# First four projection units regrouped by contraction tile, four outputs at once, two more units behind them

## Chip, cores and metric

One core of a Trainium2 chip runs the kernel. The time is that of one execution on the device in microseconds (us), as the median over runs of the same program. TensorE (PE) runs the matmuls; VectorE (DVE), ScalarE (ACT) and GpSimd (POOL) do the rest of the arithmetic, and SyncE (SP) issues the transfers from HBM.

## The reference, cut to what matters

Two requests of 256 tokens each (`x_prompt`, `x_sample`), model width 1024, pass a trunk of two layers in float32. The change touches the first steps of the layer: the RMS norm of the input and the projections of the mixers "a" (differential attention) and "b" (neighbourhood attention with a relative bias).

```python
def rmsnorm(x, g):
    x32 = x.astype(jnp.float32)
    y = x32 * lax.rsqrt(jnp.mean(x32 * x32, axis=-1, keepdims=True) + EPS)
    return (y * g.astype(jnp.float32)).astype(x.dtype)
...
    for l in range(DEPTH):
        h = rmsnorm(x, attn_norm[l])
        proj = h @ w_in[l]
        a_cols, b_cols, c_cols, d_cols, g_cols = jnp.split(proj, [p1, p2, p3, p4], axis=-1)
        ...
        o_b = natten_mixer(b_cols, b_rpb[l])
...
        x = x + merged @ w_out[l]
...
    return rmsnorm(x, final_norm)
```

## The kernel before

**Data.** x is kept transposed: eight tiles `x[d]` of 128 channels by 512 tokens (both requests side by side), all in `xall`. A projection contracts over these eight k-tiles. To keep float32 accuracy each product is made of three matmuls in the fp32r format (`mm3`, L295): high part of the weight times high part of x, high times low, low times high. `prep` (L320) makes the parts `xh` and `xl` of one tile with the norm's gain in them, `split_piece` (L278) those of the weights: ScalarE copies `raw` to `wh` (L288), VectorE makes the first half of `wl` (L291) and GpSimd the second (L292).

**Units.** The weights are laid out as a list of pieces (`_piece_order`, L128), and the main loop at the end of `trunk_kernel` goes through one unit for each piece. In layer 0 it starts bq0, bk0, bq1, bk1 (queries and keys of mixer b, 24 matmuls of 128x512 each), vb0, vb1 (values of b, whose 96 matmuls `psvb` follow in unit vb1), then aq0, ak0, aq1, ak1 and so on through gates, output projection and feed-forward. A unit's step emits its matmuls, then evacuations of earlier units, then the split of the piece two units ahead (`LOOK`) and the load of the piece three further (`RAW_BUFS`). Three buffers each stand for `raw`, `wh` and `wl`, so a piece's `wh` waits for the matmuls of the piece three before it.

**Side work.** Generators run between the units: `norm_gen` (L359) makes the norm's row: `st` (sum of squares by TensorE, L344), a chain of small steps `ms`, `ny`, `nt` on 128x4 (`newton`, L304), `rs`, the transposes `rb` (L357), and the copy `rsrow` (L372). The gain is in `xh`, but the row factor is applied when outputs are evacuated (`b_evac`, L596, makes `bc`, its high and low part; `a_evac`, L583, rotates with `cosr` and `sinr` as well, using a shuffle, GpSimd's `rsh`, and `rc`). `sq_acc` (L331) makes the squares, added up by VectorE. `bias_gen` (L698) loads the relative bias in 16 transfers and adds the mask on GpSimd (L704). `pair_gen` (L811) makes an attention pair: scores `sc` (L744), softmax on VectorE and ScalarE (`sb`, `mx`, `ri`), transposes `pt`, output `po`; the tables START, GAP and the lags say at which unit which step stands.

**Start.** SP loads x tile 0, the halves of piece 0, x tile 1, the halves of piece 1, the other x tiles in pairs, piece 2, and the constants (L1136 to L1144); nine matmuls on zeros (`warm`, L1131) run before the first weights are there. Piece 0's `wl` is made by GpSimd alone, piece 1's in quarters by both.

**PSUM.** Four banks (`pm`) for the units, two (`psx`) for scores, one (`pst`) for `pt`, one (`pso`) for `st`, `rb` and `po`.

**Order.** A scheduler orders the instructions of each engine; each engine then goes through its own in order, and an instruction whose wait isn't over holds all behind it on that engine.

Of the kernel before, what the change touches and what calls it, by code (L numbers as in the profile page):

```python
# [37 lines left out]
START = {"a": ("ak0", 7), "b": ("bk0", 4), "c": ("cv", 6), "d": ("vf1", 2)}  # L38
# [40 lines left out]
def _layout_weights(w_in, c_w_uq, c_w_ukv, w_branch, w_out, w_ffn_in, w_ffn_out):  # L79
# [5 lines left out]
    for l in range(DEPTH):  # L85
        p = {}
        for nm, cols in _col_blocks():
            a = kt(w_in[l][:, cols])
            if nm[0] == "v":
                p[nm + "0"] = a[:, 0:4]  # L90
                p[nm + "1"] = a[:, 4:8]
            else:
                p[nm] = a
        z = np.zeros((128, 2, 384), np.float32)
# [33 lines left out]
def _piece_order():  # L128
# [3 lines left out]
    names += qk[0] + [f"v{two_[0]}0", f"v{two_[0]}1"]  # L132
    rest = {"x": qk[1], "w": [f"v{two_[1]}0", f"v{two_[1]}1"], "d": ["vd0", "vd1", "ve0", "ve1"], "c": ["vf0", "vf1"]}
# [68 lines left out]
def trunk_kernel(ctx: ExitStack, tc: tile.TileContext, xt, wflat, gains, lams, rpb, consts, yt):  # L202
# [75 lines left out]
    def split_piece(i, parts=1, pool_only=False):  # L278
# [7 lines left out]
        for q in range(parts):  # L286
            a, b = q * w, q * w + w
            S.activation(out=wh[:, a:b], in_=raw[:, a:b], func=AF.Copy)  # L288
            c = a if pool_only else (a + b) // 2
            if c > a:  # L290
                V.tensor_tensor(out=wl[:, a:c], in0=raw[:, a:c], in1=f(wh[:, a:c]), op=ALU.subtract)  # L291
            G.tensor_tensor(out=wl[:, c:b], in0=raw[:, c:b], in1=f(wh[:, c:b]), op=ALU.subtract)  # L292
# [65 lines left out]

    def norm_gen(wait, rope):  # L359
# [6 lines left out]
        yield  # L366
        pb = psum("rb", pso)
# [62 lines left out]
    units = []  # L430
# [4 lines left out]
    def build_layer(l):  # L435
# [136 lines left out]
        def lin(nm, m=128):  # L572
            def pe(wh, wl):
                ps = psum("ps" + nm)
# [486 lines left out]
        for nm in ("aq0", "ak0", "aq1", "ak1"):  # L1061
            specs[nm] = (lin(nm), a_evac(nm))
# [4 lines left out]
        for nm in ("bq0", "bk0", "bq1", "bk1"):  # L1067
            specs[nm] = (lin(nm), b_evac(nm))
# [18 lines left out]
        at(1, bias_gen)  # L1087
# [24 lines left out]
        xw = 2 if l == 0 else 1  # L1112
        units[u0]["side"].append((0, lambda: norm_gen(xw, True)))
        for nm in names[:1 + xw]:
            units[u0 + pos[nm]]["nb"] = u0 + 1 + xw
# [157 lines left out]
```

## Time and profile before

| | |
|---|---|
| median of 3 runs | 1627.73 us (1627.72 to 1628.39) |
| profiled execution, own time | 1629.04 us |
| its span, first to last instruction | 1627.3 us |
| TensorE busy | 1610.2 us (99%) |
| VectorE busy | 962.9 us (59%) |
| ScalarE busy | 620.5 us (38%) |
| GpSimd busy | 661.2 us (41%) |
| mean granted TensorE clock | 0.995 |
| TensorE's share of the chain that ended last | 97% |

The span runs from the first to the last instruction of the profiled execution; its own time, measured outside, is 1.7 us longer. A granted clock of 1.00 is TensorE's upper level (2.4 GHz), 0.50 the lower (1.2 GHz). Matmuls overlap in the rows of the trace, so the distance between starts, not the listed duration, is what one costs. In the rows, "[3.39 <-ACT wh L288]" is the idle time of the engine just before the instruction and the instruction that ended it.

### The profile page before, as it was taken

Reading aid. Unit: us, or ns where it says so; the run is one execution under the profiler, and the core shown is the slowest. Engines: PE = TensorE matmul, PEld = TensorE weight load, DVE = VectorE, ACT = ScalarE, POOL = GpSimd, SP = SyncE. Lnnn points to the kernel's source line nnn. Section 1 sums busy time; section 2 is a strip of 40 time slices with the busy share of each in tenths; the row PEclk is TensorE's granted clock in tenths of the full one; section 3 lists DMA queues with packets and bytes.
Section 4 is the critical chain, followed back from the end, with each engine's and each line's share of the span. In section 5 each row is a group of like instructions: output and inputs, shape, how many; then the busy total and the mean of one; then the engine's idle time right before and its main releaser. Section 6 shows DMA issues by size and latency. Waiting matters only on the chain.

```text
span 1627.3 us, 21327 instructions
## 1 busy us (share of the span) xinstructions
PE 1610.2 (99%) x8163; PEld 1336.7 (82%) x8163; DVE 962.9 (59%) x1580; ACT 620.5 (38%) x1107; POOL 661.2 (41%) x449
## 2 busy tenths in 40 slices
PE   8999999999999999999999999999999999999997
PEld 6898788888888888888888977888788888888886
DVE  7767485656876665633366665756468656665113
ACT  4446354333333333322234555434332333333221
POOL 4432223445534444444445231244455344444342
PEclk9999999999999999999999999999999999999999
DMA  6213122221322322223332222222222222322331
GB/s 220 101 53 98 56 98 82 81 78 59 116 91 91 104 95 98 90 95 105 102 105 85 67 88 72 82 86 76 81 78 104 92 95 99 104 91 86 105 96 64
DMA packets 50534, 149.25 MB, mean 92 GB/s; under 512 B 13184, under 2 KB 16128, under 8 KB 50432
## 3 DMA queue, kind: packets, MB, share of 16 engines
q1 hardware_dynamic: 49344, 146.84, 26.8%
q8 instruction: 64, 1.05, 0.3%
q10 hardware_dynamic: 1088, 1.05, 0.2%
q14 instruction: 38, 0.31, 0.1%
HBM read 145.77 MB, written 2.10 MB: 91 GB/s over the span
## 4 chain that ended last, share of the span: by engine, by line
PE 97%; DVE 1%; ACT 1%; issue 1%; DMA 0%; POOL 0%; SPq 0%; POOLq 0%; ACTq 0%
PE pf L296 10%; PE pf L297 10%; PE pf L298 10%; PE pg L296 7%; PE pg L297 7%; PE pg L298 7%; PE pfo L296 5%; PE pfo L297 5%; PE pfo L298 5%; PE po L842 2%; PE pt L787 2%; PE pb L298 2%; PE pwo L296 2%; PE pb L297 2%; PE pb L296 2%; PE pwo L298 2%
## 5 line engine op out<-in xcount | busy, mean ns | idle before, releaser
L292 POOL TENSOR_TENSOR wl<-raw,wh 128x512 fp32r<-128x512 f32 (+4 forms) x264 | 454.4, 1723 | 567.6 <-ACT wh L288 466.6
L288 ACT ACTIVATE wh<-raw 128x1024 fp32r<-128x1024 f32 (+5 forms) x264 | 281.6, 1067 | 437.4 <-PE pfo L297 128.2
L291 DVE TENSOR_TENSOR wl<-raw,wh 128x512 fp32r<-128x512 f32 (+4 forms) x262 | 258.9, 988 | 227.6 <-ACT wh L288 209.8
L296 PE MATMUL pf<-xh,wh 128*128 128x512 f32 x704 | 274.3, 390 | 0.0
L298 PE MATMUL pf<-xh,wl 128*128 128x512 f32 x704 | 273.9, 389 | 0.0
L297 PE MATMUL pf<-xl,wh 128*128 128x512 f32 x704 | 273.9, 389 | 0.0
L296 PE MATMUL pg<-xh,wh 128*128 128x512 f32 x512 | 203.4, 397 | 0.4
L297 PE MATMUL pg<-xl,wh 128*128 128x512 f32 x512 | 199.7, 390 | 0.0
L298 PE MATMUL pg<-xh,wl 128*128 128x512 f32 x512 | 199.7, 390 | 0.0
L296 PEld LDWEIGHTS pf<-xh,wh 128*128 128x128 f32 x704 | 132.2, 188 | 27.4
L298 PEld LDWEIGHTS pf<-xh,wl 128*128 128x128 f32 x704 | 132.2, 188 | 27.4
L297 PEld LDWEIGHTS pf<-xl,wh 128*128 128x128 f32 x704 | 132.2, 188 | 27.3
L296 PE MATMUL pfo<-ah,wh 128*128 128x512 f32 (+1 forms) x374 | 141.1, 377 | 0.0
L297 PE MATMUL pfo<-al,wh 128*128 128x512 f32 (+1 forms) x374 | 140.8, 376 | 0.0
L298 PE MATMUL pfo<-ah,wl 128*128 128x512 f32 (+1 forms) x374 | 140.8, 376 | 0.0
L911 POOL TENSOR_TENSOR mg<-mg,gz 128x512 f32<-128x512 f32 x48 | 64.4, 1346 | 165.5 <-DVE gz L910 165.5
L302 POOL TENSOR_TENSOR al<-fc,ah 128x512 fp32r<-128x512 f32 x44 | 57.8, 1315 | 178.9 <-ACT ah L301 178.9
L296 PEld LDWEIGHTS pg<-xh,wh 128*128 128x128 f32 x512 | 96.2, 188 | 23.4 <-issue 1.3
L298 PEld LDWEIGHTS pg<-xh,wl 128*128 128x128 f32 x512 | 96.1, 188 | 20.7
L297 PEld LDWEIGHTS pg<-xl,wh 128*128 128x128 f32 x512 | 96.3, 188 | 18.4
L932 ACT ACTIVATE gz<-gz 128x512 f32<-128x512 f32 x64 | 40.3, 630 | 133.9 <-DVE gz L931 133.8
L767 ACT ACTIVATE pr<-sc,mx 128x256 f32<-128x256 f32 x128 | 59.0, 471 | 73.5 <-DVE mx L762 73.5
(386 smaller groups left out, 2841.5 us busy)
## 6 DMA issues: line engine op xcount, KB each, us to landing
raw<-in_w_dram SPq DMA_DIRECT2D x158, 512.0 KB, 3.2
raw<-in_w_dram SPq DMA_DIRECT2D x58, 640.0 KB, 3.8
raw<-in_w_dram SPq DMA_DIRECT2D x32, 448.0 KB, 3.2
raw<-in_w_dram SPq DMA_DIRECT2D x4, 576.0 KB, 3.3
bias<-in_rpb_dram SPq DMA_DIRECT2D x32, 64.0 KB, 3.0
xall<-in_xt_dram SPq DMA_DIRECT2D x3, 512.0 KB, 7.4
raw<-in_w_dram SPq DMA_DIRECT2D x4, 256.0 KB, 4.8
out_dram<-y SPq DMA_DIRECT2D x4, 256.0 KB, 2.4
```

The lines of the kernel that those rows point to most:

```text
L288: S.activation(out=wh[:, a:b], in_=raw[:, a:b], func=AF.Copy)
L291: V.tensor_tensor(out=wl[:, a:c], in0=raw[:, a:c], in1=f(wh[:, a:c]), op=ALU.subtract)
L292: G.tensor_tensor(out=wl[:, c:b], in0=raw[:, c:b], in1=f(wh[:, c:b]), op=ALU.subtract)
L296: PE.matmul(ps, lhsT=wh, rhs=xh, start=first, stop=False)
L297: PE.matmul(ps, lhsT=wh, rhs=xl, start=False, stop=False)
L298: PE.matmul(ps, lhsT=wl, rhs=xh, start=False, stop=last)
L302: (eng or V).tensor_tensor(out=l, in0=v, in1=f(h), op=ALU.subtract)
L767: S.activation(out=p[:, qt * 256:qt * 256 + 256], in_=src[c][:, qt * 256:qt * 256 + 256], func=AF.Exp, scale=sc, bias=mx[:, i:i + 1], accu ...
L787: PE.transpose(out=ps[:, kt * 256 + qt * 128:kt * 256 + qt * 128 + 128], in_=p[:, qt * 256 + kt * 128:qt * 256 + kt * 128 + 128], identity ...
L842: PE.matmul(ops[64 * e:64 * e + 64, :256], lhsT=v_of(mix, j, e, 2 * b + kt), rhs=pt[:, kt * 256:kt * 256 + 256], start=(kt == 0), stop=(kt ...
L911: G.tensor_tensor(out=m, in0=m, in1=z, op=ALU.add)
L932: S.activation(out=z, in_=z, func=AF.Tanh, scale=0.5)
```

## The change

The weights of bq0, bk0, bq1 and bk1 are laid out anew as four slabs. A slab holds two k-tiles of all four outputs (2 x 4 blocks of 128 columns), so that its 24 matmuls add to four PSUM banks in turn, and every k-tile of x is used for 12 matmuls as soon as it is there. Loads at the start alternate between a tile of x and half a slab, 256 KB each; cst comes in two transfers. aq0 and ak0 move up to right behind the slabs, with their outputs in `pst` and `pso`; vb0 and vb1 follow. Slabs 0 to 3 have their `wl` made by VectorE alone, in two halves. The squares are made at the start and added by VectorE into one sum. In layer 0 `norm_gen` is replaced by two hooks: `st` and the small chain at the last matmul of slab 3, `rb` and `rsrow` behind the sixth k-tile of aq0. All four outputs of the slabs are evacuated together. The bias moves from unit 1 to unit 4 in layer 0; the steps of the pairs of a and b move with START. Layer 1 has the same pieces and the same order of units, but keeps `norm_gen` and the bias at unit 1.

```diff
--- before.py
+++ after.py
@@ -35,7 +35,8 @@
 GAP = {"a": 3, "b": 2, "c": 2, "d": 3}
-START = {"a": ("ak0", 7), "b": ("bk0", 4), "c": ("cv", 6), "d": ("vf1", 2)}
+START = {"a": ("ak0", 9), "b": ("bk0", 5), "c": ("cv", 6), "d": ("vf1", 2)}
+SLAB = ["bq0", "bk0", "bq1", "bk1"]
 CLAG = 1
@@ -83,14 +84,18 @@
     for l in range(DEPTH):
-        p = {}
+        p, slab = {}, {}
         for nm, cols in _col_blocks():
...
                 p[nm + "1"] = a[:, 4:8]
+            elif nm in SLAB:
+                slab[nm] = a
             else:
                 p[nm] = a
+        for q, nm in enumerate(SLAB):
+            p[nm] = np.stack([slab[b][:, k] for k in (2 * q, 2 * q + 1) for b in SLAB], axis=1)
         z = np.zeros((128, 2, 384), np.float32)
@@ -129,8 +134,9 @@
     qk = [[f"{m}q0", f"{m}k0", f"{m}q1", f"{m}k1"] for m in two_]
-    names += qk[0] + [f"v{two_[0]}0", f"v{two_[0]}1"]
-    rest = {"x": qk[1], "w": [f"v{two_[1]}0", f"v{two_[1]}1"], "d": ["vd0", "vd1", "ve0", "ve1"], "c": ["vf0", "vf1"]}
+    assert qk[0] == SLAB
+    names += qk[0] + qk[1][:2] + [f"v{two_[0]}0", f"v{two_[0]}1"]
+    rest = {"x": qk[1][2:], "w": [f"v{two_[1]}0", f"v{two_[1]}1"], "d": ["vd0", "vd1", "ve0", "ve1"], "c": ["vf0", "vf1"]}
     for ch in 'xdcw':
@@ -275,7 +281,7 @@
 
-    def split_piece(i, parts=1, pool_only=False):
+    def split_piece(i, parts=1, only=None):
         if i >= len(order):
@@ -286,10 +292,11 @@
             S.activation(out=wh[:, a:b], in_=raw[:, a:b], func=AF.Copy)
-            c = a if pool_only else (a + b) // 2
+            c = b if only is V else (a + b) // 2
             if c > a:
                 V.tensor_tensor(out=wl[:, a:c], in0=raw[:, a:c], in1=f(wh[:, a:c]), op=ALU.subtract)
-            G.tensor_tensor(out=wl[:, c:b], in0=raw[:, c:b], in1=f(wh[:, c:b]), op=ALU.subtract)
+            if b > c:
+                G.tensor_tensor(out=wl[:, c:b], in0=raw[:, c:b], in1=f(wh[:, c:b]), op=ALU.subtract)
         splits[i] = (wh, wl)
@@ -356,6 +363,17 @@
 
+    def norm_parts(rope):
+        def stats():
+            ps = psum("st", pso)
+            main_stats(ps)
+            main_newton(ps)
+
+        def row():
+            for _ in norm_row(rope):
+                pass
+        return stats, row
+
     def norm_gen(wait, rope):
@@ -364,6 +382,9 @@
         yield
+        yield from norm_row(rope)
+
+    def norm_row(rope):
         pb = psum("rb", pso)
@@ -427,7 +448,7 @@
 
-    units = []
+    units, hooks = [], {}
 
@@ -569,15 +590,34 @@
 
-        def lin(nm, m=128):
+        def lin(nm, m=128, pool=pm):
             def pe(wh, wl):
-                ps = psum("ps" + nm)
+                ps = psum("ps" + nm, pool)
                 D[nm] = ps
...
                     mm3(ps[:m], w[0][:, k], w[1][:, k], st["xh"][k], st["xl"][k], k == 0, k == 7)
+                    if k == 5 and pool is pst and "row" in hooks:
+                        hooks.pop("row")()
+            return pe
+
+        def slab_pe(q):
+            def pe(wh, wl):
+                if q == 0:
+                    swap_h()
+                    for nm in SLAB:
+                        D[nm] = psum("ps" + nm)
+                w = [a[:, :1024].rearrange("p (k c) -> p k c", k=8) for a in (wh, wl)]
+                kb = [(k, b) for k in range(2) for b in range(4)]
+                if q == 3:
+                    kb.sort(key=lambda t: t[1])
+                for k, b in kb:
+                    d = 2 * q + k
+                    mm3(D[SLAB[b]], w[0][:, 4 * k + b], w[1][:, 4 * k + b], st["xh"][d], st["xl"][d], d == 0, d == 7)
+                    if q == 3 and (k, b) == (1, 3) and "stats" in hooks:
+                        hooks.pop("stats")()
             return pe
@@ -1059,13 +1099,14 @@
         for nm in ("aq0", "ak0", "aq1", "ak1"):
-            specs[nm] = (lin(nm), a_evac(nm))
+            specs[nm] = (lin(nm, pool={"aq0": pst, "ak0": pso}.get(nm, pm)), a_evac(nm))
         for nm, n, ev in (("va", 256, v_evac(vA)), ("vb", 256, v_evac(vB)), ("vd", 256, vd_evac), ("ve", 288, ve_evac),
...
             specs[nm + "0"], specs[nm + "1"] = (pe0, None), (pe1, None)
-        for nm in ("bq0", "bk0", "bq1", "bk1"):
-            specs[nm] = (lin(nm), b_evac(nm))
+        evs = [b_evac(nm) for nm in SLAB]
+        for q, nm in enumerate(SLAB):
+            specs[nm] = (slab_pe(q), (lambda: [e() for e in evs]) if q == 3 else None)
         specs["cq"] = (cq_pe, None)
@@ -1084,7 +1125,7 @@
 
-        at(1, bias_gen)
+        at(4 if l == 0 else 1, bias_gen)
         s = 0
@@ -1109,10 +1150,10 @@
         units[u0 + pos["fu0"]]["side"].append((0, lambda: norm_gen(1, False)))
-        xw = 2 if l == 0 else 1
-        units[u0]["side"].append((0, lambda: norm_gen(xw, True)))
-        for nm in names[:1 + xw]:
-            units[u0 + pos[nm]]["nb"] = u0 + 1 + xw
+        if l == 0:
+            hooks["stats"], hooks["row"] = norm_parts(True)
+        else:
+            units[u0]["side"].append((0, lambda: norm_gen(1, True)))
         units[u0 + pos["wo0"]]["nb"] = u0 + pos["wo1"] + 1
@@ -1133,32 +1174,46 @@
     xv = xt.rearrange("(d p) t -> p d t", p=128)
-    nc.sync.dma_start(out=xall[:, 0:1], in_=xv[:, 0:1])
-    load_piece(0, 2)
-    nc.sync.dma_start(out=xall[:, 1:2], in_=xv[:, 1:2])
-    load_piece(1, 2)
-    for a, b in ((2, 4), (4, 6), (6, 8)):
-        nc.sync.dma_start(out=xall[:, a:b], in_=xv[:, a:b])
-    load_piece(2)
-    nc.sync.dma_start(out=cst, in_=consts)
+
+    def load_slab(i):
+        raw = wpool.tile([128, 1280], F32, tag="raw", name=f"raw{i}", bufs=RAW_BUFS)
+        src = wflat[offs[i]:offs[i] + 128 * 1024].rearrange("(p n) -> p n", p=128)
+        for q in range(2):
+            d = 2 * i + q
+            nc.sync.dma_start(out=xall[:, d:d + 1], in_=xv[:, d:d + 1])
+            nc.sync.dma_start(out=raw[:, q * 512:q * 512 + 512], in_=src[:, q * 512:q * 512 + 512])
+        raws[i] = raw
+
+    for i in range(3):
+        load_slab(i)
+    nc.sync.dma_start(out=cst[:, K_ID:], in_=consts[:, K_ID:])
+    prep(0, gcol(0, G_ATTN), False)
+    split_piece(0, 2, V)
+    load_slab(3)
+    nc.sync.dma_start(out=cst[:, :K_ID], in_=consts[:, :K_ID])
     nc.sync.dma_start(out=lv, in_=lams.rearrange("(u n) -> u n", u=1).to_broadcast([128, DEPTH * L_ROW]))
-    prep(0, gcol(0, G_ATTN), False)
-    split_piece(0, 2, True)
-    load_piece(RAW_BUFS)
+    accs = []
+
+    def sq_start(d):
+        sq = t2(f"sq{d}")
+        S.activation(out=sq, in_=x[d], func=AF.Square)
+        if d:
+            V.tensor_tensor(out=accs[0], in0=accs[0], in1=sq, op=ALU.add)
+        else:
+            accs.append(sq)
+
     for d in range(1, ND):
-        prep(d, gcol(0, G_ATTN + d), False, d % 2 == 1)
+        prep(d, gcol(0, G_ATTN + d), False, True)
         if d == 2:
-            split_piece(1, 2)
+            split_piece(1, 2, V)
             load_piece(1 + RAW_BUFS)
-
-    def sq_gen():
-        for d in range(ND):
-            sq_acc(d, d)
-            if d in (2, 4):
-                yield
-        yield
-
-    units[0]["side"].insert(0, (0, sq_gen))
+        if d >= 3:
+            sq_start(d - 3)
+            if d == ND - 1:
+                for e in range(d - 2, ND):
+                    sq_start(e)
+    st["accs"] = accs
+
     for i in range(2, LOOK):
@@ -1206,7 +1261,7 @@
         vec(1)
-        split_piece(i + LOOK)
+        split_piece(i + LOOK, *((2, V) if i + LOOK < 4 else ()))
         load_piece(i + LOOK + RAW_BUFS)
```

The first place is TensorE at the first real matmuls. Names end in the piece or k-tile (`xh1` is the high part of the second tile of x, `wh0` that of piece 0) and, behind the underscore, a running number. Before:

```order
L296 MATMUL psbq0_180<-xh0_122,wh0_126 128x512
L297 MATMUL psbq0_180<-xl0_123,wh0_126 128x512
L296 MATMUL psbk0_247<-xh0_122,wh1_142 128x512
L297 MATMUL psbk0_247<-xl0_123,wh1_142 128x512
L298 MATMUL psbk0_247<-xh0_122,wl1_143 128x512
L296 MATMUL psbk0_247<-xh1_134,wh1_142 128x512
L298 MATMUL psbq0_180<-xh0_122,wl0_127 128x512
L296 MATMUL psbq0_180<-xh1_134,wh0_126 128x512
L297 MATMUL psbq0_180<-xl1_135,wh0_126 128x512
L298 MATMUL psbq0_180<-xh1_134,wl0_127 128x512
L297 MATMUL psbk0_247<-xl1_135,wh1_142 128x512
L298 MATMUL psbk0_247<-xh1_134,wl1_143 128x512
```

After the change:

```order
L303 MATMUL psbq0_199<-xh0_123,wh0_127 128x512
L304 MATMUL psbq0_199<-xl0_124,wh0_127 128x512
L303 MATMUL psbk0_200<-xh0_123,wh0_127 128x512
L304 MATMUL psbk0_200<-xl0_124,wh0_127 128x512
L305 MATMUL psbq0_199<-xh0_123,wl0_128 128x512
L305 MATMUL psbk0_200<-xh0_123,wl0_128 128x512
L303 MATMUL psbq1_201<-xh0_123,wh0_127 128x512
L304 MATMUL psbq1_201<-xl0_124,wh0_127 128x512
L305 MATMUL psbq1_201<-xh0_123,wl0_128 128x512
L303 MATMUL psbk1_202<-xh0_123,wh0_127 128x512
L304 MATMUL psbk1_202<-xl0_124,wh0_127 128x512
L305 MATMUL psbk1_202<-xh0_123,wl0_128 128x512
```

Before, the third matmul already needs piece 1 (`wh1`); now the first twelve use piece 0 and x tile 0 alone, over four outputs.

The second place is VectorE at the norm of layer 0, `wl` being halves of weight splits. Before, from the end of the small chain on:

```order
L352 COPY rs_330<-ny_315 128x4
L376 TENSOR_TENSOR rs2_371<-rs_330 128x4
L1173 TENSOR_REDUCE lp_395<-lv_84 128x1 x4
L291 TENSOR_TENSOR wl5_412<-raw5_216,wh5_411 128x512
L1177 TENSOR_TENSOR lam_85<-lp_395 128x1 x2
L1179 TENSOR_SCALAR lam_85<-lam_85 128x1 x2
L372 COPY rsrow_369<-rb_339 128x512
L601 TENSOR_TENSOR bc_377<-psbq0_180,rsrow_369 128x8x64
```

After the change, from inside the chain:

```order
L314 TENSOR_SCALAR ny_329<-ny_329 128x4
L318 TENSOR_TENSOR nt_330<-ny_329 128x4
L319 TENSOR_TENSOR nt_330<-nt_330,nh_331 128x4
L297 TENSOR_TENSOR wl6_456<-raw6_265,wh6_455 128x512
L320 SCALAR_TENSOR_TENSOR ny_329<-nt_330,ny_329 128x4
L318 TENSOR_TENSOR nt_330<-ny_329 128x4
L319 TENSOR_TENSOR nt_330<-nt_330,nh_331 128x4
L320 SCALAR_TENSOR_TENSOR ny_329<-nt_330,ny_329 128x4
```

and from its end:

```order
L1232 TENSOR_TENSOR lam_85<-lp_346 128x1 x2
L1234 TENSOR_SCALAR lam_85<-lam_85 128x1 x2
L297 TENSOR_TENSOR wl7_498<-raw7_296,wh7_497 128x512
L393 COPY rsrow_413<-rb_408 128x512
L641 TENSOR_TENSOR bc_427<-psbq0_199,rsrow_413 128x8x64
L309 TENSOR_TENSOR bq0l_430<-bc_427,bq0h_429 128x512
```

A split (`wl6`) stands inside the small chain now, and `wl7`, not `wl5`, is the split ahead of `rsrow`; `wl7` uses the buffer of piece 4, which is aq0.

TensorE there, after the change:

```order
L364 MATMUL rb_408<-cst_82,rs_344 128x128 x4
L303 MATMUL psaq0_389<-xh6_176,wh4_291 128x512
L304 MATMUL psaq0_389<-xl6_177,wh4_291 128x512
L305 MATMUL psaq0_389<-xh6_176,wl4_292 128x512
L303 MATMUL psaq0_389<-xh7_183,wh4_291 128x512
L304 MATMUL psaq0_389<-xl7_184,wh4_291 128x512
L305 MATMUL psaq0_389<-xh7_183,wl4_292 128x512
L303 MATMUL psak0_462<-xh0_123,wh5_362 128x512
```

ak0 (`psak0`) follows aq0 and `rb` directly, in the bank that `rb` used.

The third place is VectorE behind the four evacuations, at the first scores (`sc_`, read by `sb`). Before:

```order
L291 TENSOR_TENSOR wl6_425<-raw6_281,wh6_424 128x512
L302 TENSOR_TENSOR bk1l_421<-bc_418,bk1h_420 128x512
L755 SCALAR_TENSOR_TENSOR sb_552<-sc_431,bias0_227 128x512
L755 SCALAR_TENSOR_TENSOR sb_596<-sc_432,bias1_232 128x512
L761 TENSOR_REDUCE mx_549<-sb_552 128x2
```

After the change, first the part up to the softmax's first step:

```order
L297 TENSOR_TENSOR wl8_541<-raw8_367,wh8_540 128x512
L309 TENSOR_TENSOR bk1l_448<-bc_445,bk1h_447 128x512
L627 TENSOR_TENSOR rc_487<-psaq0_389,cosr_417 128x512
L628 STREAM_SHUFFLE rsh_488<-psaq0_389 128x512
L630 TENSOR_TENSOR rc_487<-rc_487,rsh_488 128x512
L309 TENSOR_TENSOR aq0l_494<-rc_487,aq0h_493 128x512
L795 SCALAR_TENSOR_TENSOR sb_521<-sc_504,bias0_369 128x512
L627 TENSOR_TENSOR rc_530<-psak0_462,cosr_417 128x512
L801 TENSOR_REDUCE mx_518<-sb_521 128x2
```

and the part up to the second:

```order
L630 TENSOR_TENSOR rc_530<-rc_530,rsh_531 128x512
L810 RECIPROCAL ri_520<-su_519 128x2
L817 TENSOR_SCALAR sb_521<-sb_521,ri_520 128x256 x2
L309 TENSOR_TENSOR ak0l_537<-rc_530,ak0h_536 128x512
L795 SCALAR_TENSOR_TENSOR sb_654<-sc_505,bias1_374 128x512
```

Before, the two `sb` on bias0 and bias1 stood side by side behind `bk1l`; now the evacuation of aq0 stands ahead of the first, and that of ak0 and the first softmax ahead of the second.

## Rows read from the trace of the kernel before

**Rows 1.** Waits of TensorE over the span: who waits, releaser, us, times, longest.

```profile
PE rb L357 <- DVE rs L352: 1.0, 1, 1.0
...
PE sc L744 <- DVE bk0l L302: 0.4, 1, 0.4
```

**Rows 2.** Windows, columns: stretch, its us, each engine's busy, PEclk, DMA share, GB/s.

```profile
8.00:9.00 1.00, 0.00 (x0) 0.00 (x0) 0.20 (x1) 0.95 (x2) 0.23 (x1) 0.56 0.90 336
9.00:14.00 5.00, 4.66 (x10) 3.31 (x11) 4.93 (x8) 3.02 (x5) 1.64 (x2) 0.50 1.05 409
...
15.00:21.00 6.00, 6.00 (x28) 4.96 (x27) 5.86 (x12) 5.84 (x10) 1.61 (x1) 1.00 0.79 281
```

**Rows 3.** Order of time on TensorE: start, us, line, out<-in, count, [idle, releaser].

```profile
5.22 0.50 PE L296 MATMUL psbq<-xh,wh 128*128 128x512 f32 x1
5.55 0.40 PE L297 MATMUL psbq<-xl,wh 128*128 128x512 f32 x1
9.34 0.80 PE L296 MATMUL psbk<-xh,wh 128*128 128x512 f32 x1 [3.39 <-ACT wh L288]
...
18.14 0.39 PE L296 MATMUL psbq<-xh,wh 128*128 128x512 f32 x1
18.36 0.39 PE L297 MATMUL psbk<-xl,wh 128*128 128x512 f32 x1
...
26.39 1.02 PE L344 MATMUL st<-cst,sq 128*128 128x1 f32 x8
27.27 0.48 PE L297 MATMUL psbq<-xl,wh 128*128 128x512 f32 x1
...
30.15 0.62 PE L357 MATMUL rb<-cst,rs 128*128 128x128 f32 x4
...
35.17 0.28 PE L454 MATMUL psvb<-wh,xh 128*128 128x256 f32 x1
...
54.23 0.38 PE L744 MATMUL sc<-bk0h,bq0h 64*128 64x256 f32 x2
```

**Rows 4.** Order of time on ScalarE, 8 to 30 us.

```profile
8.05 0.72 ACT L323 ACTIVATE xh<-xall,gn 128x512 fp32r<-128x512 f32 x1 [1.15 <-DMA xall<-in_xt_dram]
...
29.23 1.06 ACT L288 ACTIVATE wh<-raw 128x1024 fp32r<-128x1024 f32 x1 [5.47 <-DVE ny L313]
```

**Rows 5.** Order of time on VectorE, 4 to 62 us.

```profile
4.41 0.75 DVE L326 SCALAR_TENSOR_TENSOR xl<-xall,gn,xh 128x512 fp32r<-128x512 f32 x1
...
27.45 0.16 DVE L349 TENSOR_SCALAR ms<-st 128x4 f32<-128x4 f32 x1 [0.56 <-PE st L344]
...
33.54 0.68 DVE L372 COPY rsrow<-rb 128x512 f32<-128x512 f32 x1
...
44.00 1.28 DVE L755 SCALAR_TENSOR_TENSOR sb<-sc,bias 128x512 f32<-128x512 f32 x2
...
48.57 0.69 DVE L291 TENSOR_TENSOR wl<-raw,wh 128x512 fp32r<-128x512 f32 x1
...
55.86 0.68 DVE L755 SCALAR_TENSOR_TENSOR sb<-sc,bias 128x512 f32<-128x512 f32 x1
...
59.79 0.69 DVE L590 TENSOR_TENSOR rc<-rc,rsh 128x512 f32<-128x512 f32 x1 [1.36 <-POOL rsh L589]
...
61.79 0.68 DVE L755 SCALAR_TENSOR_TENSOR sb<-sc,bias 128x512 f32<-128x512 f32 x1
```

**Rows 6.** Order of time on VectorE in layer 1, 819 to 826 us.

```profile
819.04 1.30 DVE L306 TENSOR_SCALAR ny<-ms 128x4 int32<-128x4 int32 x1
...
823.37 1.28 DVE L311 TENSOR_TENSOR nt<-ny 128x4 f32<-128x4 f32 x1
...
825.28 0.16 DVE L376 TENSOR_TENSOR rs<-rs 128x4 f32<-128x4 f32 x1
```

**Rows 7.** Order of time on GpSimd in layer 1, 819 to 824 us.

```profile
819.02 1.30 POOL L292 TENSOR_TENSOR wl<-raw,wh 128x512 fp32r<-128x512 f32 x1 [4.04 <-ACT wh L288]
...
823.34 1.28 POOL L704 TENSOR_TENSOR bias<-bias,cst 128x512 f32<-128x512 f32 x1 [1.69 <-DVE ny L313]
```

## Prediction

> **What bounds the kernel now.** I read the waits of TensorE first, because it is busy 99% of the span (table above): what a change can win or lose is the time in which TensorE stands, or runs slowly. Inside the program three waits matter: 3.4 us at the start (the value in brackets at 9.34 [rows 3]), 0.4 us at the first scores and 1.0 us at the row broadcast of layer 1 [rows 1]. Next the windows: the granted clock is 0.56 in 8–9 us, 0.50 in 9–14 and 1.00 from 15 on [rows 2], so the first gap also costs speed behind it. Then the order of time on TensorE [rows 3]: it starts real work at 5.22, stands until 9.34 for the second unit's weights, and begins the v units at 35.17. The 96 slab matmuls, `st` and `rb` in between would take 96 x 0.23 + 0.88 + 0.62 = 23.6 us at the spacing of the rows at 18.14 and 18.36; they take 29.95. Of the 6.4 us lost, 3.4 are the gap and 3.0 the low clock. That is all that the change can win at the start. The profiled run took 1629.04 us, span 1627.3; the median of the runs is 1627.73. My sum is a difference against the profiled execution; I add it to the median, which leaves the profiled run 1.3 above.
>
> **The slab.** No matmul is added or removed; the first 96 are regrouped so that one k-tile of x and one 256 KB half of a weight piece feed 12 matmuls (2.8 us), where before a k-tile of x fed 3. k0: 5.22 to 7.98. For k1 the second half of piece 0 is now the fourth 256 KB transfer; before, the fourth was the second tile of x, whose user started at 8.05 [rows 4]. ScalarE's copy then ends about 8.7, VectorE's `wl` half takes 0.69 [rows 5], and only the third matmul of k1 needs it: at 9.45. TensorE stands about 1.0 us here, in two pieces, instead of 3.4. Then 82 x 0.23 = 18.9 us: the slab ends at 28.3. Nobody else is slower per 2.8 us: ScalarE has a gain copy (0.72), a `wh` half and a square (each bounded by the same 0.72), 2.2 in all [rows 4], VectorE an `xl` (0.75), a `wl` (0.69) and one addition (0.69 by the nearest row) = 2.1 [rows 5]; 512 KB at the 281 to 409 GB/s of the windows take 1.3 to 1.9 us [rows 2]. The squares now lie under this, on VectorE, and the split of slabs 0–3 leaves GpSimd idle, so nothing there holds VectorE. With `st` and `rb` the old content ends at 28.3 + 0.88 + 0.62 = 29.8 against 35.17: **−5.4** (between −6.4, no gap at all, and −4.4, a gap twice as long). The old 0.4 us at the first scores goes as well: before, they went on 5.2 us after `rsrow` ended; now 24 matmuls of ak0, 5.5 us, lie between. **−0.4.**
>
> On four banks in turn: the granted clock is 1.00 in 15–21 us while the matmuls alternate between two banks at 0.23 [rows 2, 3], so I charge nothing for it. The Trainium skill ("TensorE: Matmul & The Clock Gate", section "A second HAM failure mode: psum-queue depth-cycling") says that cycling through PSUM banks leaves TensorE idle for moments between groups and makes its clock oscillate. By that rule the slab would run in part at the lower level of 1.2 GHz; this trace shows nothing of it with two banks, and no run here has four. It is a rival below.
>
> **What hangs behind the slab.** Three places, all in the quoted orders.
>
> *rb.* `st` starts at 28.3 and `rs` must be ready for the `rb` transposes after `st` and 18 matmuls of aq0, at 28.3 + 0.88 + 4.14 = 33.3. Before, the small chain on VectorE began with `ms` at 27.45, 1.06 after `st`, and let `rb` go at 30.15, 2.7 later, with GpSimd idle [rows 3, 5]. Now the split of wl6 stands inside the chain, and GpSimd has its half of wl6 and two bias additions at the same time, because the bias moves from unit 1 to unit 4. Exactly these three operations stand beside the chain in layer 1, where single 128x4 steps take 1.28 to 1.30 in place of 0.16, beginning together with a GpSimd operation of 1.30, and the chain takes 6.4 from its first small step to the last [rows 6, 7]. The bounds: unheld, 28.3 + 1.06 + 2.7 + 0.7 = 32.8, no stall; held as in layer 1, 35.8, a stall of 2.5. The row in layer 1 is the nearest, but the bias transfers need not land at the worst moments: **+2.0.**
>
> *ak0.* Its output shares the single bank of pool pso with `rb`, so its first matmul waits for `rsrow`, the copy out of `rb`. On VectorE wl7 stands ahead of `rsrow`; wl7 waits for ScalarE's wh7; wh7 goes into aq0's buffer (three are there) and can start only after aq0's last matmul. So TensorE waits through a whole `wh` (1.06), a `wl` half (0.69) and `rsrow` (0.68) [rows 4, 5], with hand-over about **+2.5**. It is at least 2.4, by these durations; at most 3.5, if GpSimd begins its half first: such a VectorE half ran 1.0 us longer by the held steps [rows 6]. Before, `rsrow` stood behind wl5 too, but 24 psvb matmuls and more were free to run.
>
> *Second scores.* The second half of the second set waits for `sb` on bias1, which frees the score bank. In the new order this `sb` stands behind the evacuations of all four slab outputs and of aq0 and ak0. From the end of `rsrow` (34.22) to `sb` (44.00) before: 9.8 us for the four outputs and one split [rows 5], the same now. Then aq0's chain: 0.68 + 0.73 + a wait of 1.36 on GpSimd + 0.69 + 0.7 + 0.69 = 4.9. Then one round `sb` to `sb` as between 55.86 and 61.79: 5.9; and `sb` itself 0.7 [rows 5]. In all 21.3 us after `rsrow`. TensorE needs from there ak0 (as many matmuls as aq0), the first scores and 96 psvb matmuls: before, 35.17 to 54.23 less the 0.4 wait = 18.6 [rows 1, 3], and 0.45 for the first half: 19.1. Stall **+2.2**; between +1.2, if each of ten hand-overs is 0.1 shorter, and +3.5, if one held VectorE half of 1.3 more falls in.
>
> *Clock.* The one fall that the rows show came in the 3.4 us gap: TensorE's last matmul before it began at 5.55 and the window at 8–9 has 0.56 [rows 2, 3]. The stall at ak0 is nearly as long, so I reckon with a fall there. Low clock cost 3.0 at the start; here 2.2 of it run inside the wait at the second scores, which VectorE sets: **+0.8** net, and no second fall there. Bounds: 0 (no fall), +3.8 (a fall at `rb` too, where nothing absorbs it, or one behind the scores).
>
> In layer 1 the same pieces and order come, but its norm is made ahead with the generator and the 1.0 us wait at `rb` stays; the tail is untouched. Splitting cst and placing lv last costs nothing: their users come after 18 us. SP issues 11 more transfers, at the load rate reckoned above.
>
> **Sum.** −5.4 − 0.4 + 2.0 + 2.5 + 2.2 + 0.8 = +1.7: **1629.4 us**, a profiled run about 1630.7. Within 0.2% (3.3 us), about what a measurement of this kernel can tell from no change.
>
> **Rivals.**
> - *Nothing holds the small chain* (bias transfers land late): no stall at `rb`, −5.4 − 0.4 + 2.5 + 2.2 + 0.8 = −0.3: 1627.4. For it: GpSimd stands 1.69 before the last bias addition of layer 1 [rows 7], so its operations come in gaps; against: the same three stand there. 0.18.
> - *The start is kept*: neither `rb` nor the scores wait: −5.4 − 0.4 + 2.5 = −3.3 or better: 1624.4. It needs 2 us more speed on VectorE than the round at 55.86 shows. 0.10.
> - *The other side, clearly slower*: the chain is held in full, TensorE stands 2.5 at `rb`, the clock falls there, the last six matmuls of aq0 take 1.4 more, and wl7 runs behind GpSimd (+1.0). It decides once the stall at `rb` is as long as the one at ak0. With 2.5 for 2.0 the sum is +1.7 + 0.5 + 1.4 + 1.0 = +4.6: 1632.3. 0.22.
> - *The slab waits for data again*: if k1's weights come as late as unit 1's did, the gap and the low clock of before are back: at least 1.7 + 3.0 = +4.7: 1632.4. Against: 336 GB/s at 8–9 us [rows 2]. 0.05.
> - *The banks in turn throttle the clock*: the 82 matmuls behind k1's start at twice 0.23: +19: about 1648. Rows of two banks speak against it. 0.02.
> - My forecast: 0.43; of it some 0.03 ends above +3.3.
>
> **How the numbers follow.** Faster by over 0.2%: 0.10. Slower: 0.22 + 0.05 + 0.02 + 0.03 = 0.32. Within: 0.18 + 0.40 = 0.58. The range reaches from 1625.0 (a little above the kept start) to 1633.4 (the slower rival with 1.1 more for a held split at the scores); outside lie most of the kept start and the bank rival.
>
> **What would show it.** Right: no wait over 1 us before 28 us and a granted clock of 1.00 through 28; then waits of psak on `rsrow` of 2.4 to 3.5 us, of `rb` on `rs` of 0 to 2.5, of `sc` on `sb` of 1.2 to 3.5. Wrong: the slab ends after 30, psak does not wait, or the clock is below 1.00 inside the slab. If the three waits together are under 4 us, the start is kept and I am too slow; over 9 us, or a second stretch at 0.50 behind 55 us, I am too fast.

## The result and the profile after

The changed kernel takes 1643.29 us (median of 4 runs, 1642.87 to 1645.42) against 1628.06 for the kernel before measured with it: ratio 1.0095, 95% interval 1.0077 to 1.0112. It is 15.2 us slower; forecast were 1629.4 and a range up to 1633.4. In the profiled executions the span went from 1627.3 to 1641.4 us, 14.1 more, and this difference is taken apart here.

First where along the program it arises. The rows give, for the matmuls of the output projection, count, durations in ns (least, median, most) and the starts of the first (layer 0) and of the last (layer 1). Before:

```profile
L296 PE MATMUL pwo<-mh,wh x128: 389/389/389, 408.4 to 1252.2; 128*128 128x512 f32 x128
```

After:

```profile
L303 PE MATMUL pwo<-mh,wh x128: 389/389/390, 417.6 to 1265.8; 128*128 128x512 f32 x128
```

So 9.2 us are lost ahead of layer 0's output projection, 13.6 by that of layer 1 (4.4 more), and 0.5 behind it. My prediction had nothing for layer 1. The waits of TensorE over the whole span, after (who waits, releaser, us in total, times, longest):

```profile
PE sc L784 <- DVE sb L795: 3.8, 3, 1.9
PE rb L364 <- DVE rs L359: 3.0, 2, 2.1
...
PE psak L303 <- DVE rsrow L393: 2.2, 1, 2.2
PE sc L784 <- DVE cf L540: 1.5, 2, 0.7
```

The start, order of time on TensorE after the change (start, us, engine, line, operation, operands, count, [idle and what ended it]):

```profile
5.46 0.50 PE L303 MATMUL psbq<-xh,wh 128*128 128x512 f32 x1
...
8.55 0.50 PE L303 MATMUL psbq<-xh,wh 128*128 128x512 f32 x1
...
9.27 0.50 PE L305 MATMUL psbq<-xh,wl 128*128 128x512 f32 x1
...
18.02 0.39 PE L304 MATMUL psbk<-xl,wh 128*128 128x512 f32 x1
18.24 0.39 PE L305 MATMUL psbk<-xh,wl 128*128 128x512 f32 x1
...
27.99 0.95 PE L351 MATMUL st<-cst,sq 128*128 128x1 f32 x8
28.80 0.49 PE L303 MATMUL psaq<-xh,wh 128*128 128x512 f32 x1
...
35.33 0.62 PE L364 MATMUL rb<-cst,rs 128*128 128x128 f32 x4 [2.15 <-DVE rs L359]
...
40.45 0.77 PE L303 MATMUL psak<-xh,wh 128*128 128x512 f32 x1 [2.19 <-DVE rsrow L393]
...
63.68 0.38 PE L784 MATMUL sc<-bk0h,bq0h 64*128 64x256 f32 x1 [1.85 <-DVE sb L795]
```

The 3.4 us gap of [rows 3] is gone: k1 begins at 8.55, its `wl` part at 9.27, and the slab is done when `st` starts at 27.99 (28.3 forecast). With `st` (0.8) and `rb` (0.4, the distance from its start to that of the next matmul) the old content would be done at 29.2 in place of 35.17: 6.0 us won. Behind it stand the three forecast waits: 2.15, 2.19 and 1.85. Then the windows after the change (us, busy of PE, PEld, DVE, ACT, POOL, granted clock, DMA share, GB/s):

```profile
5.00:28.00 23.00, 22.96 (x99) 17.98 (x98) 18.37 (x29) 15.08 (x26) 3.14 (x2) 1.00 0.83 296
...
32.00:36.00 4.00, 1.85 (x11) 1.33 (x10) 3.56 (x15) 0.20 (x1) 2.03 (x2) 1.00 0.51 92
36.00:40.00 4.00, 2.27 (x6) 1.23 (x4) 1.22 (x5) 1.06 (x1) 0.94 (x1) 0.51 0.75 178
40.00:45.00 5.00, 4.55 (x11) 3.65 (x12) 3.57 (x5) 1.26 (x2) 5.00 (x5) 0.50 0.29 106
45.00:50.00 5.00, 5.00 (x29) 3.88 (x28) 2.58 (x5) 1.86 (x3) 1.78 (x2) 0.86 0.00 0
```

A granted clock between 0.50 and 1.00 is the mean of a stretch that had both levels. The clock fell behind the wait at `rb` and stayed at its lower level through most of ak0. From the first matmul behind `rb` (35.71) to the first scores (48.84), less the wait of 2.19, the 30 matmuls took 10.9 us, at 0.23 each 6.9: 3.9 us with the hand-over taken off. Up to the end of the second scores the sum is −6.0 − 0.4 + 2.15 + 2.19 + 3.9 + 1.85 = +3.7 us (64.5 us after, 60.75 before with as many matmuls done). The other 5.5 us of layer 0, and the 4.4 of layer 1, come later, at the scores of mixer a. Layer 0, TensorE after:

```profile
109.00 0.39 PE L784 MATMUL sc<-ak0h,aq0h 32*128 32x256 f32 x3
...
109.69 0.28 PE L784 MATMUL sc<-ak0h,aq0l 32*128 32x256 f32 x2
110.95 0.38 PE L784 MATMUL sc<-ak0h,aq0h 32*128 32x256 f32 x1 [0.98 <-DVE sb L795]
111.17 0.28 PE L784 MATMUL sc<-ak0l,aq0h 32*128 32x256 f32 x1
...
130.78 0.38 PE L784 MATMUL sc<-ak0h,aq0h 32*128 32x256 f32 x1 [0.73 <-DVE cf L540]
```

The same place before:

```profile
105.93 0.39 PE L744 MATMUL sc<-ak0h,aq0h 32*128 32x256 f32 x4
106.16 0.28 PE L744 MATMUL sc<-ak0l,aq0h 32*128 32x256 f32 x4
106.27 0.29 PE L744 MATMUL sc<-ak0h,aq0l 32*128 32x256 f32 x4
```

and what VectorE did at that moment, after:

```profile
110.21 0.68 DVE L795 SCALAR_TENSOR_TENSOR sb<-sc,bias 128x512 f32<-128x512 f32 x1
```

A score step of mixer a uses four banks (two of `psx`, two of `pm`) and rows of 32, and its four matmuls go together, one group each 0.12 us (x4). After the change only three banks are free: the fourth still holds the scores of b's last pair until its `sb` on bias is done at 110.9. So TensorE waits 0.98 us and then runs the fourth matmul of each group by itself. At the next step the late bank is one of `pm`: it is free when `cf`, the copy out of `psvf`, is done, and TensorE waits 0.73 us. Layer 1 shows the same in its waits:

```profile
PE sc L784 <- DVE sb L795: 1.0, 1, 1.0
PE rb L364 <- DVE rs L359: 0.8, 1, 0.8
PE sc L784 <- DVE cf L540: 0.7, 1, 0.7
PE psva L475 <- ACT pr L807: 0.3, 1, 0.3
```

1.7 us of the 4.4 there are waits at mixer a's scores, and 0.3 is one of `psva` just behind them. Added up by the distances between starts, mixer a's scores take 2.0 us more beside their waits, because groups go in parts, and the outputs `po` of the pairs 1.4 more, two of which go as 2 and 6 matmuls in place of 8; about 1.0 is won back in small amounts elsewhere. Layer 0 is alike: 2.0 in waits, 2.1 and 1.6.

### The profile page after: what moved, and what is told of

It reads as the page before. It is cut to its first block, busy times and chain, and to the rows that moved or that the text cites. A ratio compares the mean times of both kernels' runs of the same rounds, so it can differ in the third digit from the quotient of the medians.

```text
span 1641.4 us, 21354 instructions
## 1 busy us (share of the span) xinstructions
PE 1617.7 (99%) x8163; PEld 1341.9 (82%) x8163; DVE 966.2 (59%) x1581; ACT 623.0 (38%) x1112; POOL 654.1 (40%) x443
## 4 chain that ended last, share of the span: by engine, by line
PE 95%; DVE 2%; issue 1%; ACT 1%; SPq 1%; POOL 0%; DMA 0%; POOLq 0%; ACTq 0%; DVEq 0%
PE pf L303 10%; PE pf L305 10%; PE pf L304 10%; PE pg L303 7%; PE pg L304 7%; PE pg L305 7%; PE pfo L303 5%; PE pfo L305 5%; PE pfo L304 5%; PE po L882 2%; PE pt L827 2%; PE pb L305 2%; PE pwo L304 2%; PE pwo L303 2%; PE pb L304 2%; PE pb L303 2%
## 5 line engine op out<-in xcount | busy, mean ns | idle before, releaser
L299 POOL TENSOR_TENSOR wl<-raw,wh 128x512 fp32r<-128x512 f32 (+4 forms) x258 | 444.7, 1725 | 577.9 <-ACT wh L294 471.5
L297 DVE TENSOR_TENSOR wl<-raw,wh 128x512 fp32r<-128x512 f32 (+4 forms) x266 | 263.9, 992 | 225.7 <-ACT wh L294 212.6
L972 ACT ACTIVATE gz<-gz 128x512 f32<-128x512 f32 x64 | 40.3, 630 | 133.9 <-DVE gz L971 133.8
```

Of the source, the lines that this page charges most:

```text
L972: S.activation(out=z, in_=z, func=AF.Tanh, scale=0.5)
```

## The experiments

Each ran in the same series as fresh runs of the kernel before (medians 1628.25 to 1628.44); ratios are to these, with 95% intervals.

**1. The kernel before, b's pairs one unit later.**

```diff
-START = {"a": ("ak0", 7), "b": ("bk0", 4), "c": ("cv", 6), "d": ("vf1", 2)}
+START = {"a": ("ak0", 7), "b": ("bk0", 5), "c": ("cv", 6), "d": ("vf1", 2)}
```

> The kernel before, with one number changed: the four pairs of mixer b start one unit later (unit 6, 8, 10, 12 in place of 5, 7, 9, 11), mixer a at unit 14 as before, in both layers. Theory crowding: the 4.4 us that the changed kernel loses in layer 1, and about as much between 65 and 146 us of layer 0, come from this shift alone, since it moves b's last pair to within two units of a's first. Then this kernel loses 3 to 5 us per layer, 6 to 10 us in all (1634 to 1638), and TensorE waits for sb and cf at the scores of mixer a show in both layers. Rival order: the loss comes from the new places of aq0 and ak0 or of their evacuations. Then this kernel stays within 2 us of 1628 and shows no such waits.

Measured: 1643.68 us, ratio 1.0092 (1.0077 to 1.0107). One number in the old kernel costs 15.3 us, as much as the whole change, though not in the same places: the first `pwo` starts at 415.0 and the last at 1267.3, so 6.6 us are lost in layer 0 and 8.5 in layer 1. That the two totals agree is chance. Its waits:

```profile
PE po L842 <- ACT ptr L793: 3.0, 2, 2.0
...
PE sc L744 <- DVE sb L755: 1.9, 2, 1.0
...
PE sc L744 <- DVE cf L519: 1.5, 2, 0.7
```

The waits on `sb` and `cf` are those of the changed kernel, 1.0 and 0.7 in each layer. It lost more than the 6 to 10 expected: `po` waits on `ptr` as well, and in layer 1 the clock fell twice between 911 and 941 us (a mean of 0.83 in two windows of 10 us), which the changed kernel doesn't show there. The shift alone is enough to make these waits; crowding holds, its size was set too low.

**2. The changed kernel, b's pairs where they were.**

```diff
-START = {"a": ("ak0", 9), "b": ("bk0", 5), "c": ("cv", 6), "d": ("vf1", 2)}
+START = {"a": ("ak0", 9), "b": ("bk0", 4), "c": ("cv", 6), "d": ("vf1", 2)}
```

> The changed kernel with b's pairs at units 5, 7, 9, 11 as in the kernel before, nothing else changed. Theory crowding: the waits of the scores of mixer a on sb and cf (1.0 and 0.7 us in each layer) and the parted score groups vanish in both layers: 4.4 us each, so about 1634 to 1636; the waits at rb and at ak0 (2.2 us each) stay. Rival order: within 2 us of 1643, the waits stay.

Measured: 1634.42 us, ratio 1.0037 (1.0022 to 1.0051), 8.9 less than the changed kernel. The waits on `cf` are gone, none of mixer a's scores waits, and those at `rb` (2.1) and ak0 (2.2) stay. The output projection shows that both layers gain:

```profile
L303 PE MATMUL pwo<-mh,wh x128: 389/389/389, 412.5 to 1257.7; 128*128 128x512 f32 x128
```

Of the 9.2 us lost ahead of it in layer 0, 4.1 are left, and of the 4.4 in layer 1, 1.3; there a score of b now waits 0.9 on `sb`.

**3. The changed kernel, the last pair of b alone earlier (units 6, 8, 10, 11).**

```diff
-                    s += GAP[mix]
+                    s += 1 if mix == "b" and (j, b) == (1, 0) else GAP[mix]
```

> The changed kernel with b's pairs at units 6, 8, 10, 11 in both layers: only the last of the four is one unit earlier (11 in place of 12, where it was before the change). Theory crowding: what costs the 4.4 us per layer is the distance of b's last pair to a's first (units 12 and 14); then the waits of mixer a's scores on sb and cf vanish here as in after_b_earlier, 8 us fewer than 1643.3, about 1635. Rival: the later start of all four counts (the evacuations of aq1 and ak1 meet them), the waits stay and the total is over 1640.

Measured: 1636.98 us, ratio 1.0054 (1.0040 to 1.0068): 6.3 of the 8.9 come back by the last pair alone. No score of mixer a waits; a wait of 1.0 us of `pt` on `ptr` in each layer is new, which I put down to the two pairs that are now close, without having tried it. So it is the distance between b's last pair and a's first that counts for most of it.

**4. The changed kernel, bias of layer 0 at unit 2.**

```diff
-        at(4 if l == 0 else 1, bias_gen)
+        at(2 if l == 0 else 1, bias_gen)
```

> The changed kernel with the bias loads and additions of layer 0 at unit 2 in place of unit 4; the scheduler then also puts rsrow ahead of the split of piece 7 on VectorE. Theory: the stall at rb comes from GpSimd's bias additions beside the small chain and the stall at ak0 from the split ahead of rsrow, and these two stalls are what lets the clock fall. Then the wait at rb falls from 2.2 to 0.5 or less, the wait at ak0 from 2.2 to 0.7 or less, the granted clock stays at 1.00 from 28 to 50 us, and the time falls by 2.2 + 2.2 + 4.1 (low clock) less what the wait at the second scores takes back (up to 4): 4 to 8 us, 1635 to 1639. Rival chain: the small chain is slow by itself or held by the split of piece 6; then the wait at rb stays over 1.5 us and the clock still falls.

Measured: 1639.84 us, ratio 1.0069 (1.0054 to 1.0084), 3.5 less than the changed kernel. `rb` waits 1.07 us, ak0 not at all, and the clock is 1.00 from 28 to 55 us. Half a miss: 1.07 is left at `rb`, since one bias addition and GpSimd's half of piece 6 still run beside the small chain and hold two of its steps (1.24 and 1.21 us); the second scores now wait 2.76 us, psvb 1.52 on a split, and behind the scores the clock falls (a mean of 0.68 from 60 to 65 us), so more was handed back than I expected.

**5. Edits 2 and 4 together.**

```diff
+START = {"a": ("ak0", 9), "b": ("bk0", 4), "c": ("cv", 6), "d": ("vf1", 2)}
...
+        at(2 if l == 0 else 1, bias_gen)
```

> Both edits: b's pairs at units 5, 7, 9, 11 and the bias of layer 0 at unit 2. If both theories hold the gains add up: 1643.3 less 8.8 less 4 to 8: 1626 to 1631, at or below the kernel before, because the 6.2 us won in the slab are then kept in part. Rival: the gains do not add (the earlier scores meet the same evacuations), and it stays above 1633.

Measured: 1629.34 us (10 runs), ratio 1.0005 (0.9996 to 1.0014): no difference from the kernel before. The gains add up, and a little over: 8.9 and 3.5 singly, 13.95 together.

**6. The norm's `st` and `rb` in a bank of the scores' pool.** ak0 then has its bank from the start.

```diff
-            ps = psum("st", pso)
+            ps = psum("st", psx)
...
-            for _ in norm_row(rope):
+            for _ in norm_row(rope, psx):
...
-        pb = psum("rb", pso)
+        pb = psum("rb", pool)
```

> The changed kernel with st and rb of layer 0 in a bank of the scores' pool, so that ak0 has the bank of pso from the start; all else as changed. Theory: the 2.2 us wait of ak0 on rsrow vanishes, that of rb on rs (2.2) stays. If the clock falls from the wait at rb by itself, the stretch at 36 to 46 us stays at 0.50 and the total is about 1641; if it took both waits together, the granted clock stays at 1.00 there. In both cases the second scores wait longer, since VectorE's chain behind rsrow is not shortened: 1638 to 1642, so less than 2.2 + 4 us are won. Rival: the second scores do not wait longer, and 1637 or less is measured.

Measured: 1644.17 us, ratio 1.0098 (1.0083 to 1.0113); nothing is won. Its waits and windows:

```profile
PE sc L784 <- DVE sb L795: 4.4, 3, 2.5
PE rb L364 <- DVE rs L359: 2.9, 2, 2.1
...
PE sc L784 <- DVE bk0l L309: 1.3, 1, 1.3
```

```profile
36.00:40.00 4.00, 4.00 (x20) 3.27 (x19) 1.98 (x5) 1.06 (x1) 1.81 (x2) 1.00 0.62 171
60.00:65.00 5.00, 2.51 (x11) 1.88 (x10) 4.96 (x9) 1.18 (x2) 1.29 (x1) 0.92 0.48 163
65.00:70.00 5.00, 5.00 (x16) 3.90 (x15) 2.79 (x9) 1.53 (x5) 0.00 (x0) 0.50 0.15 60
```

ak0's wait is gone and `rb` still waits 2.1, yet the clock doesn't fall there; so that wait alone does not always bring it down. TensorE then meets VectorE's chain: 1.3 us on bk0l, 2.5 on the second `sb`, and the clock falls behind that. The second scores go on at 64.27 (63.68 in the changed kernel): the wait of ak0 was cover for a chain on VectorE that ends when it ends. A further fall, a mean of 0.83 from 110 to 120 us, comes at mixer a's scores, where the changed kernel has the same waits and a clock of 1.00.

**7. The slabs alone, the next two units back in their old places and banks** (layer 1 as before the change, the pairs of a and b where they were, the bias of layer 0 at unit 2).

```diff
-    names += qk[0] + qk[1][:2] + [f"v{two_[0]}0", f"v{two_[0]}1"]
+    names += qk[0] + [f"v{two_[0]}0", f"v{two_[0]}1"]
...
-            specs[nm] = (lin(nm, pool={"aq0": pst, "ak0": pso}.get(nm, pm)), a_evac(nm))
+            specs[nm] = (lin(nm, pool=pm), a_evac(nm))
...
```

> Only the slabs, with their loads, squares and splits, in layer 0; aq0 and ak0 go back behind vb0 and vb1 into the four pm banks, b's and a's pairs start where they did before, the bias is loaded at unit 2, and layer 1 has the pieces and the order of the kernel before. Theory banks: the slab ends at 28 us as in the changed kernel, but the v matmuls need a pm bank, and the first comes free only after rb, rsrow and the first bc, so TensorE stands from 29 to about 35 us with a fall of the clock behind it: psvb starts at 35 to 36 (35.2 before), and the total is 1629 to 1632, nothing gained from the slab. Rival: the two more units behind the slab are not needed, psvb starts before 32 and the total is 1622 to 1625.

Measured: 1632.24 us, ratio 1.0024 (1.0014 to 1.0034), just over the 1629 to 1632 expected.

```profile
PE rb L365 <- DVE rs L360: 5.3, 1, 5.3
PE psvb L476 <- DVE bc L642: 1.6, 1, 1.6
```

With all four banks held by the slab, TensorE stands 6.9 us, psvb starts at 37.25 (35.17 before), and the clock is 0.50 from 33 to 40. The two units behind the slab are what covers the norm; without them the slab is a loss.

**8. Experiment 5 with layer 1 as in the kernel before** (pieces, banks, order, norm; the slab in layer 0 alone).

```diff
-    return [(l, nm) for l in range(DEPTH) for nm in names]
+    late = names[:4] + names[6:8] + names[4:6] + names[8:]
+    return [(l, nm) for l in range(DEPTH) for nm in (names if l == 0 else late)]
...
```

> As after_both (b's pairs at units 5, 7, 9, 11, bias of layer 0 at unit 2), but layer 1 has the pieces, banks, norm and order of the kernel before; the slab is made in layer 0 alone. Theory: the 0.9 us wait at the second scores of layer 1 and the parted score groups there (6.3 us for the 64-row scores in place of 4.5) go away: 1.8 us less than after_both, about 1627.5. Rival: layer 1 is equal in both, 1629.3.

Measured: 1627.95 us (10 runs), ratio 0.9997 (0.9988 to 1.0007). 1.4 less than experiment 5, where 1.8 was expected; the two intervals overlap.

**9. The same, bias of layer 0 at unit 1.**

```diff
-        at(2 if l == 0 else 1, bias_gen)
+        at(1 if l == 0 else 1, bias_gen)
```

> As layer1_as_before, with the bias of layer 0 at unit 1: its loads go ahead of those of piece 6, so the split of piece 6 also leaves the small chain on VectorE. Theory: the 1.1 us wait left at rb is the split of piece 6 and GpSimd's half of it; it falls under 0.3 and the total to about 1626.5. Rival: the weights of vb0 and vb1 come too late behind the bias loads; psvb waits over 1 us and nothing is gained.

Measured: 1625.81 us (10 runs, 1625.29 to 1626.13), ratio 0.9984 (0.9975 to 0.9994). This one beats the kernel before, by 2.4 us. Its waits:

```profile
PE sc L786 <- DVE sb L797: 1.2, 2, 0.7
...
PE rb L366 <- DVE rs L361: 0.9, 1, 0.9
PE sc L786 <- ACT bk0h L310: 0.4, 1, 0.4
```

The 0.9 on `rs` is layer 1's; `rb` in layer 0 no longer waits. With the split of piece 6 and the bias out of the small chain it isn't held: from `ms` at 29.11 to `rs` it has no step over 0.17 us.

**10. Experiment 9 with b's pairs of layer 0 at 6, 8, 10, 11.**

```diff
-START = {"a": ("ak0", 9), "b": ("bk0", 4), "c": ("cv", 6), "d": ("vf1", 2)}
+START = {"a": ("ak0", 9), "b": ("bk0", 5), "c": ("cv", 6), "d": ("vf1", 2)}
...
-                    s += GAP[mix]
+                    s += 1 if l == 0 and mix == "b" and (j, b) == (1, 0) else GAP[mix]
```

> layer1_as_before_bias1 with b's pairs of layer 0 at units 6, 8, 10, 11 in place of 5, 7, 9, 11. The first scores then stand behind all of ak0 and do not wait for bk0 (0.4 us); the second scores come one unit later, so the two waits on sb (0.7 and 0.5) and the parted score groups with them should shrink. Theory: 1 to 2 us less, about 1624.5. Rival: pairs at 10 and 11 meet each other at the two score banks, with waits of the scores on sb at 85 to 100 us, and nothing or a loss is measured.

Measured: 1630.24 us, ratio 1.0011 (1.0002 to 1.0020), a miss. The first scores don't wait now, but the second wait 2.76 us on `sb`, and the windows show a mean of 0.83 from 56 to 66: I read it as TensorE running into the chain in one long stop. By then some 2.7 of the 4.7 us between its profile and that of experiment 9 are lost. The rest comes near a's first scores, as the rival had it, though not by a wait of scores on `sb`: `pt` waits 0.98 us at 106 us, as in experiment 3.

**11. Experiment 9 with the low parts of pieces 7 to 9 made by GpSimd alone.**

```diff
-            c = b if only is V else (a + b) // 2
+            c = b if only is V else a if only is G else (a + b) // 2
...
-        split_piece(i + LOOK, *((2, V) if i + LOOK < 4 else ()))
+        split_piece(i + LOOK, *((2, V) if i + LOOK < 4 else (1, G) if 7 <= i + LOOK < 10 else ()))
```

> layer1_as_before_bias1 with the low parts of pieces 7, 8 and 9 of layer 0 made by GpSimd alone (about 2.6 us each), which takes three splits of 0.67 to 1.6 us off VectorE between 40 and 50 us. Theory: the waits of the second scores on sb (0.7 and 0.5) are VectorE's chain; it gets 2 us shorter, and the total falls by 1 to 2 us to about 1624.5. Rival: GpSimd's longer operations hold VectorE's steps and its own rsh comes later; no gain or a loss, and psvb or psaq may wait for wl.

Measured: 1626.59 us, ratio 0.9990 (0.9981 to 0.9999), not better than experiment 9. One wait on `sb` went, psvb waits 0.5 on GpSimd's `wl`, and the granted clock has a mean of 0.83 from 46 to 56.

## Why the prediction was wrong, step by step

**The slab: right.** 6.0 us won, 5.4 forecast; 0.2 of the 0.6 is that I took the duration of `rb`'s row (0.62) for its cost. The granted clock is 1.00 from 5 to 28 us while four banks take turns, and the matmuls follow each other at 0.23 (18.02 to 18.24), so the rival by the banks falls. The Trainium skill ("TensorE: Matmul & The Clock Gate", section "A second HAM failure mode: psum-queue depth-cycling") tells of a kernel in which TensorE stood for moments between the groups of matmuls while it cycled through banks, and its clock oscillated. Here TensorE was busy for 22.96 of the 23.00 us, and no such loss shows.

**rb: right.** 2.15 for 2.0. VectorE's small steps beside GpSimd's operations, after:

```profile
29.17 1.24 DVE L313 TENSOR_SCALAR ny<-ms 128x4 int32<-128x4 int32 x1
...
31.54 1.25 DVE L320 SCALAR_TENSOR_TENSOR ny<-nt,ny 128x4 f32<-128x4 f32 x1
...
33.02 1.17 DVE L319 TENSOR_TENSOR nt<-nt,nh 128x4 f32<-128x4 f32 x1
```

```profile
29.10 1.29 POOL L299 TENSOR_TENSOR wl<-raw,wh 128x512 fp32r<-128x512 f32 x1 [4.03 <-ACT wh L294]
31.03 3.15 POOL L744 TENSOR_TENSOR bias<-bias,cst 128x512 f32<-128x512 f32 x2 [0.64 <-DMA bias<-in_rpb_dram]
```

Three steps are held, one by each operation, as in [rows 6, 7]. The wait goes with the number of held steps: 2.15 with three here, 1.07 with two in experiment 4, none in experiment 9, where none is held.

**ak0: right.** 2.19 for 2.5, by the split ahead of `rsrow`; experiment 4 turns the two round and the wait is gone.

**Second scores: right in size, wrong in what hides there.** 1.85 for 2.2. But I let low clock behind ak0 run inside this wait ("+0.8 net"); the clock fell behind `rb`, 3.9 us were lost, and the wait stayed, because VectorE's own chain also came later than I reckoned (from `rsrow`'s end at 40.3 to the end of the second `sb` at 63.6: 23.3 us, not 21.3). The 2.0 us more lie in the four outputs of the slabs (11.9 us to the first step of aq0's evacuation, 9.8 forecast). A `bk1l` and a `bk0l` that took 1.79 and 1.63 beside GpSimd's operations are in it, but two such halves were in the row from before as well:

```profile
37.70 1.64 DVE L302 TENSOR_TENSOR bk0l<-bc,bk0h 128x512 fp32r<-128x512 f32 x1 [0.70 <-ACT bk0h L301]
...
41.84 1.63 DVE L291 TENSOR_TENSOR wl<-raw,wh 128x512 fp32r<-128x512 f32 x1
```

New, after the change, is that VectorE stands for the split of piece 8 ahead of `bk1l`. Its `wh` goes into the buffer of ak0, and ScalarE could begin it only behind ak0's last matmul, which the low clock had made late:

```profile
49.86 0.69 DVE L297 TENSOR_TENSOR wl<-raw,wh 128x512 fp32r<-128x512 f32 x1 [1.72 <-ACT wh L294]
```

```profile
48.77 1.06 ACT L294 ACTIVATE wh<-raw 128x1024 fp32r<-128x1024 f32 x1 [1.96 <-PE psak L304]
```

So the low clock did not only run beside VectorE's chain, it held that chain up as well. That step is 3.1 us short.

**The step that failed: "In layer 1 the same pieces and order come, but its norm is made ahead with the generator and the 1.0 us wait at `rb` stays; the tail is untouched."** It and my sum count nothing behind the second scores. START moves b's pairs from units 5, 7, 9, 11 to 6, 8, 10, 12, while a stays at 14 (7 + 7 before, 5 + 9 after). I read that line of the diff as following the units that had moved, and never asked where b's last pair then meets a's first. It cost 5.5 us in layer 0 and 4.4 in layer 1: 9.9 of the 14.1. Experiment 1 makes the same waits with that number alone in the old kernel; experiments 2 and 3 take them away, and 2 gives back 8.9 us. The signs by which I meant to know that I was right (the slab, the clock in it, the three waits) came, psak's wait 0.2 under its bounds; all of them lie ahead of 65 us, where these 9.9 had not begun.

With the start's gain and stalls as measured (+3.7), this sum would have been 1631.8 on the median of 1628.06, inside the range; the crowding took it out. The rival for slower had the right first link (the clock falls at `rb`) and gave 1632.3.

## What to carry to other kernels

When a change moves units in a list, write out the steps of every generator that is tied to them, in old and new positions, and look at the distance of neighbours that share banks: one unit nearer cost more here than all the waits at the place of the change. A wait on the critical engine that covers another engine's chain is worth nothing when it alone is removed (experiment 6); the chain behind it has to be shortened first. A chain of very short VectorE steps is best kept free of large GpSimd operations in its few microseconds.

## What had not been expected of the hardware

- The same wait of 2.1 us at `rb` was followed by a granted clock of 0.51 in the changed kernel (36 to 40 us) and of 1.00 in experiment 6. What decides between the two was not tried.
- The clock also fell, to a mean of 0.83 over 10 us, behind waits of 0.54 and 0.65 us that ended at 44.55 and 45.71 (experiment 11, 46 to 56 us), and behind one of 0.97 (experiment 1, 911 to 921 us). The changed kernel has a wait of the same length at the same scores and a clock of 1.00 from 911 to 921 us. Part of the 15.3 us of experiment 1 is this; how large it is from run to run was not measured.
- Four matmuls on 32 rows each, in four banks, cost one step of 0.12 us together; if one bank is late, the late one costs a step of its own in all six groups, beside the wait.
